# Weight parts in plain rows, read by the matmuls in passes over groups of eight or four

## The chip, the cores and the metric

The kernel runs on one core of a Trainium2 chip. The metric is the device time of one execution in microseconds; the median over several runs is compared. The trace and the page come from one profiled execution of the kernel before the change.

## The reference

With the sizes of this case (DEPTH = 1) only layer 0 and the last norm are computed: an RMS norm, a projection to q, k, v and gate, stick-breaking attention in 32 heads of 128, a gated output projection with a residual, and a final RMS norm. x is 256 x 4096, w_in 4096 x 16384, w_out 4096 x 4096, all float32.

```
def reference(x, norm_attn, w_in_attn, w_out_attn, ..., final_norm):
    h = x + attn_branch(rms_norm(x, norm_attn), w_in_attn, w_out_attn)
    return rms_norm(h, final_norm)

def attn_branch(xn, w_in, w_out):
    q, k, v, g = jnp.split(xn @ w_in, 4, axis=-1)
    o = stick_breaking_attention(to_heads(q), to_heads(k), to_heads(v))
    return (o * jax.nn.silu(g)) @ w_out

# per head, scores z = q k^T / sqrt(128), strictly causal:
#   log_a = log_sigmoid(z) + sum over later keys j < t of log_sigmoid(-z_tj)
#   o = exp(log_a) @ v
```

## The kernel before

**Numbers in two parts.** Every float32 operand of the two large projections is split into a high part (rounded to the float32r kind that the tensor engine takes in one pass) and a low part, the rest. `mm3` multiplies high x high, high x low and low x high: one *product* is three matmuls that add into the same PSUM bank. The activations (128 x 128 blocks, tiles sh and sl for the input side, oh and ol for the output side) are the stationary operand; a weight part (128 rows x 512 columns, tiles wh and wl) is the moving one.

**Units, steps, parts.** The work is cut into 20 units of 16 steps. Units 0 to 15 are the input projection (each gives two heads), units 16 to 19 the output projection. A step covers 256 rows of the reduction (two chunks of 128, c = 0 and 1) and two quadruples of column blocks. Units 0 and 16 are "plain" and make 8 products a step; the others save multiplications as in Strassen's scheme, with 7 products in ten of the steps (`SEVEN`) and 8 in the others. The sums of weight blocks that this needs are made by VectorE in place and by DMAs that add into the raw tiles (issued on POOL). In all there are 2383 products, 7149 matmuls of 512 columns.

**How a weight part is made.** SyncE loads a raw tile (`load`); ScalarE casts it to the high part and VectorE subtracts to get the low part (`piece`, `minus`). There are 7 raw tiles, 7 high and 5 low slots of full size, and two slots for singles, in which one chunk is formed and its high and low parts lie together.

**How a part lies and is read.** With `by_runs` a part of 1024 elements a partition lies in the order (h c i e): 64 groups h, in each the two chunks c, in each the two column blocks i, and last a run e of four elements. A matmul takes one chunk: it reads the runs of four that are 64 bytes apart, first all of block 0, then all of block 1, and writes its bank in order. Chunk 1 starts 32 bytes after chunk 0.

**What orders the work.** `Plan` is a simulated clock that the program runs while it is built: each engine has a queue of ready items with keys (due times), and an item is emitted when its engine is free in the simulation. So the order of instructions on every engine follows from cost formulas such as `tensor_ns` and `vector_ns`. `PRODUCT` is three times the tensor cost of 512 columns. The matmuls of the heads (transposes, scores, sums along a row, output) go through `ten`, between the products, with a key that puts them first.

**The output units.** `blocks_of_heads` forms the stationary parts of the output projection from the spilled results of the heads: it loads a block p on POOL's queue, casts it and subtracts. `later_than`, with SPREAD, says behind which step of the last input unit or of unit 16 each of these may begin.

Of the kernel before, what the change touches and what calls it, by code (L numbers as in the profile page):

```python
# [11 lines left out]
F32R = mybir.dt.float32r  # L12
# [7 lines left out]
P = 128  # L20
# [6 lines left out]
HG = CW // P  # L27
NB = D // CW
W = 2 * CW
NJ = D // W  # L30
KT = 2
NS = KC // KT
EPS = 1e-6

RUN = 4
WARM, IDLE = 10, 640


# [9 lines left out]
LOWS = 5  # L48
# [6 lines left out]
KEPT = 5  # L55
LAST_ORDER = (5, 4, 2, 3)

SPREAD = (12, 1.0)
HEADS_AHEAD = 0
SUMS_LATER = 2  # L60
H_LATER = 6
# [40 lines left out]


def tensor_ns(n):
    return 0.4167 * n + 12.4 if n > 128 else 109.0


class Plan:
# [135 lines left out]
def kernel(  # L244
# [10 lines left out]
    nc = Plan(tc)  # L255
# [3 lines left out]
    wp = ctx.enter_context(tc.tile_pool(name="weights", bufs=1))  # L259
# [10 lines left out]
    def minus(out_, full, part):  # L270
        nc.vector.tensor_tensor(out=out_, in0=full, in1=part.bitcast(F32), op=ALU.subtract)
# [30 lines left out]
    for b in LAST_ORDER:  # L302
        order += [(n, k) for n in kept for k, prod in enumerate(parts[n]["prods"]) if prod[0] == b]
    starts, ends, first, left, place_of = {}, {}, {}, {}, {}
    PRODUCT = 3 * tensor_ns(W)
    for g, (n, k) in enumerate(order):
        p = parts[n]
        b = p["u"], p["prods"][k][0]
# [16 lines left out]
    def dve(emit, n, key=None, more=0, **kw):  # L325
        n = n if isinstance(n, tuple) else (n,)
        cost = sum(vector_ns(m) for m in n) + 122 * (len(n) - 1) + more
        return nc.work("vector", cost, emit, soon() if key is None else key, **kw)

    def act(emit, n, key=None, **kw):  # L330
        n = n if isinstance(n, tuple) else (n,)
        cost = sum(scalar_ns(m) for m in n) + 100 * (len(n) - 1)
        return nc.work("scalar", cost, emit, soon() if key is None else key, **kw)


    FULL_P, FULL_S = (P,) * 2, (W,) * 2

    def ten(emit, *n):
        return nc.work("tensor", 40 + sum(tensor_ns(m) for m in n), emit, nc.here - 1e4, wait=400)

    def moved(engine, emit, sizes, key, after=None, hold=False, adds=False, wait=0):
        issue = 550 if engine == "gpsimd" else 330
# [17 lines left out]
    raw, wh, wl = {}, {}, {}  # L360
# [44 lines left out]
    def low_done(n):  # L405
        lows_left[n] -= 1
        if not lows_left[n]:
            nc.tell(("lows", n))
            tile_done(*parts[n]["tile"])

    def sums(q):

        a, b, c, d = quad_parts[q]
        one, two = raw[q, 0], raw[q, 1]
        for k in range(2):
            tile_left[q, k] += 1

        def add(to, at_, f, g, key, op=ALU.add):
            return dve(
                lambda: nc.vector.tensor_tensor(out=to[:, :, at_, :], in0=f, in1=g, op=op), W,  # L420
                key - SUMS_AHEAD * 1e3, more=120 if op == ALU.subtract else 10,
            )

        yield nc.until(("lows", a), ("T3", q))
        yield add(one, 0, one[:, :, 0, :], two[:, :, 0, :], first[c], ALU.subtract)
        yield nc.until(("lows", b))
        yield add(two, 1, one[:, :, 0, :], two[:, :, 1, :], first[c])
        nc.tell(("sums", c))
        yield add(one, 1, one[:, :, 0, :], one[:, :, 1, :], first[d])
        nc.tell(("sums", d))  # L430
        for k in range(2):
            tile_done(q, k)

    def by_runs(t):

        return t.rearrange("p (h c i e) -> p c i h e", c=KT, i=HG, e=RUN)

    def piece(n, c, there):

        p = parts[n]  # L440
        yield nc.until(*there)
        full = raw[p["tile"]][:, :, p["place"], :][:, :, c, :].rearrange("p i c (h e) -> p c i h e", e=RUN)
        h = wh[n][:, c]
        size = (c.stop - c.start) * W
        key = first[n] - (AHEAD * 1e3 if p["seven"] and p["i"] < 2 else 0)
        yield act(lambda: nc.scalar.copy(h, full), size, key - 2.0 * 1e3)
        if p["size"] == KT:
            if c.start == 0:
                yield nc.take("wl")
                wl[n] = by_runs(wp.tile([P, KT * W], F32R, tag="wl", name=f"wl{n}", bufs=LOWS))  # L450
                nc.tell(("lowslot", n))
            else:
                yield nc.until(("lowslot", n))
        l = wl[n][:, c]
        if n == 0:
            yield nc.until(("sh", c.start))
        yield dve(lambda: minus(l, full, h), size, key, more=10)
        for k in range(c.start, c.stop):
            nc.tell(("low", n, k))
        low_done(n)  # L460

    def split(size, tag, bufs):
        for n, p in enumerate(parts):
            if p["size"] != size:
                continue
            q = p["quad"]
            t = p["tile"][1]
            if size == KT:
                yield nc.take(tag)
            yield nc.until(("raw", q, t))  # L470
            if size < KT:
                yield nc.take(tag)
            wh[n] = by_runs(wp.tile([P, KT * W], F32R, tag="wh" if size == KT else "s", name=f"wh{n}", bufs=bufs))
            if size == 1:
                wh[n], wl[n] = wh[n][:, 0:1], wh[n][:, 1:2]
            cuts = [slice(k, k + 1) for k in range(KT)] if n == 0 else [slice(0, size)]
            lows_left[n] = len(cuts)
            if p["seven"] and p["i"] == 0:
                nc.start(sums(q))
            for c in cuts:  # L480
                nc.start(piece(n, c, [("sums", n)] if p["seven"] and p["i"] > 1 else [("raw", q, t)]))
# [312 lines left out]
        nc.give("gh")  # L794
        nc.tell(("gate", u))

    def mm3(out_, a, b, start, stop):

        (ah, al), (bh, bl) = a, b
        if len(bh.shape) == 4:  # L800
            out_ = out_.rearrange("p (i h e) -> p i h e", i=HG, e=RUN)
        kw = dict(skip_group_check=True)
        nc.tensor.matmul(out_, ah, bh, start=start, stop=False, **kw)
        nc.tensor.matmul(out_, ah, bl, start=False, stop=False, **kw)
        nc.tensor.matmul(out_, al, bh, start=False, stop=stop, **kw)


    BW = 3 * P
# [5 lines left out]
    def head(u, i):  # L814
# [3 lines left out]
        def turn():  # L818
            for k in range(2):
                for t in range(NT):  # L820
                    c = k * CW + i * P
                    nc.tensor.transpose(tr[:, k, t * P : (t + 1) * P], st["qk", u][:, t, c : c + P], ident)

        yield ten(turn, P, P, P, P)
        if i == HG - 1:
            nc.give("one")
# [6 lines left out]
        def scores():  # L833
            kw = dict(stop=False, skip_group_check=True)
            nc.tensor.matmul(z[:, 0:P], qk[:, 1, P:S], qk[:, 0, P:S], start=True, **kw)
            nc.tensor.matmul(z[:, P:BW], qk[:, 1, 0:P], qk[:, 0, :], start=False, **kw)

        yield ten(scores, *FULL_P, *FULL_S)
        nc.give("gh")
        yield nc.take("gh")  # L840
# [20 lines left out]
        def scan():  # L861
# [4 lines left out]
            nc.tensor.matmul(z[:, 2 * P : BW], neg_one, fl[:, 0:P], stop=True, **kw)  # L866

        yield ten(scan, BW, BW, P, P)
        nc.give("gh", "gh")
        yield nc.take("gh")  # L870
# [70 lines left out]
    def later_than(u, s):  # L941
        s = int(SPREAD[0] + SPREAD[1] * s)
        return "used", u + s // NS, s % NS
# [282 lines left out]
            nc.tell(("used", u, s))  # L1226

    def product(n, k):
        p = parts[n]
        b, f, c = p["prods"][k]  # L1230
        h, l = forms[p["s"]]
        mm3(
            ev[p["u"]][b],
            (h[:, PLACES[f], :], l[:, PLACES[f], :]),
            (wh[n][:, c], wl[n][:, c]),
            starts[p["u"], b] == (n, k),
            ends[p["u"], b] == (n, k),
        )

    def products():  # L1240
        for g, (n, k) in enumerate(order):
            p = parts[n]
            u, s = p["u"], p["s"]
            b, f, c = p["prods"][k]
            if u < 1:
                what = "s"
            elif u < OUT0:
                what = "n"
            elif u == OUT0:
                what = "o"  # L1250
            else:
                what = "r" if u == LAST and s in EIGHT_LAST else "p"
            if starts[u, b] == (n, k):
                yield nc.take(f"b{b}")
                ev.setdefault(u, {})[b] = acc.tile([P, W], F32, tag=f"b{b}", name=f"acc{u}_{b}")
            yield nc.until(("low", n, c), ("form", what, s), lead=nc.LEAD)
            yield nc.work(
                "tensor", PRODUCT, lambda: product(n, k), g * PRODUCT, after=lambda n=n, k=k: done(n, k), hold=False
            )
            nc.here = g * PRODUCT  # L1260

    together(split(KT, "w", HIGHS), split(1, "s", SINGLES), products(), x_stats(), x_factor(), constants())

    def in_turn(works):
# [55 lines left out]
```

## Time and profile before

| | |
|---|---|
| median of 3 runs | 1725.65 us (1722.67 to 1726.70) |
| the profiled execution | 1725.08 us, of which the span of its instructions is 1722.3 us |
| granted TensorE clock | 0.998 |
| busy: PE, PEld, DVE, ACT, POOL | 99%, 82%, 95%, 70%, 19% of the span |
| moved by DMA | 413.82 MB, mean 240 GB/s |

PE is the tensor engine's matmuls, PEld its weight loads, DVE VectorE, ACT ScalarE, POOL GpSimd. Matmuls overlap in the profile, since each begins before the one ahead has ended; the distance between two starts tells more than a duration. All of the kernel's operations are recorded through one helper, so they all stand under its line, L127, and are told apart by their tiles: wh and wl are the weight's parts, sh, sl, oh and ol the stationary blocks, acc the banks, raw the loaded weights, qk_sb, gv_sb, z, f and a the heads' tiles, p the spilled results that come back.

### The profile page before, as it was taken

What the parts mean: (1) busy time and instruction counts of PE and PEld (TensorE: products, weight loads), DVE (VectorE), ACT (ScalarE), POOL (GpSimd) and SP (SyncE); (2) the same over time, 40 slices, a digit from 0 to 9 for tenths busy, and PEclk for the clock granted to TensorE, in tenths of its full rate; (3) what the DMA queues carried; (4) which work ended last, traced back from release to release, by engine and by line L of the source; (5) the groups of instructions that cost most, each with busy time, mean ns of one, the idle gap of its engine ahead of it and who ended that gap; (6) DMA issues with size and microseconds to landing.
All of it is one profiled execution on the core that took longest, in us unless ns stands there. A gap on an engine that the chain in (4) does not pass through costs nothing. (4 is left out here: it accounts for less than half of the span.)

```text
span 1722.3 us, 25298 instructions
## 1 busy us (share of the span) xinstructions
PE 1704.4 (99%) x7735; PEld 1415.7 (82%) x7735; DVE 1634.9 (95%) x2106; ACT 1199.3 (70%) x1640; POOL 335.6 (19%) x407
## 2 busy tenths in 40 slices
PE   9999999999999999999999999999999999999997
PEld 7888888888888888888888888888888888878786
DVE  8899999999999999999999999999999978999997
ACT  8986767676767676767676767676767765666655
POOL 0012222222222222121212121212222112122120
PEclk9999999999999999999999999999999999999999
DMA  9978787878787979797978787878788978898895
GB/s 342 329 199 234 220 248 221 247 215 259 206 264 197 266 194 273 191 270 199 266 202 257 207 249 216 245 214 245 221 238 224 278 243 253 232 258 248 242 301 196
DMA packets 249384, 413.82 MB, mean 240 GB/s; under 512 B 28128, under 2 KB 73440, under 8 KB 249248
## 3 DMA queue, kind: packets, MB, share of 16 engines
q1 hardware_dynamic: 194544, 354.24, 62.2%
q0 software_dynamic: 54416, 57.70, 20.4%
q8 instruction: 60, 0.98, 0.2%
q14 instruction: 76, 0.62, 0.1%
q10 hardware_dynamic: 288, 0.28, 0.0%
HBM read 403.98 MB, written 8.13 MB: 239 GB/s over the span
## 5 line engine op out<-in xcount | busy, mean ns | idle before, releaser
L127 ACT CAST wh<-raw 128x1024 fp32r<-128x1024 f32 (+1 forms) x995 | 922.3, 969 | 412.2 <-DVE raw L127 207.3
L127 DVE TENSOR_TENSOR wl<-raw,wh 128x1024 fp32r<-128x1024 f32 (+1 forms) x818 | 974.9, 1218 | 33.7 <-PE acc L127 13.5
L127 PE MATMUL acc<-wh,sh 128*128 128x512 f32 x2048 | 783.5, 394 | 1.1 <-DVE qk_sb L127 0.7
L127 PE MATMUL acc<-wh,sl 128*128 128x512 f32 x1898 | 733.3, 386 | 0.0
L127 PE MATMUL acc<-wl,sh 128*128 128x512 f32 x1748 | 675.3, 386 | 0.0
L127 POOL DMA_DIRECT2D raw<-in_w_in_dram x300 | 263.1, 996 | 977.8 <-DMA raw<-in_w_in_dram 326.5
L127 PEld LDWEIGHTS acc<-wh,sh 128*128 128x128 f32 x2048 | 384.1, 188 | 77.9 <-issue 2.2
L127 PEld LDWEIGHTS acc<-wh,sl 128*128 128x128 f32 x1898 | 356.1, 188 | 73.4 <-DVE sl L127 0.5
L127 PEld LDWEIGHTS acc<-wl,sh 128*128 128x128 f32 x1748 | 328.5, 188 | 61.5 <-DVE wl L127 0.4
L127 DVE TENSOR_TENSOR raw<-raw,raw 128x512 f32<-128x512 f32 x354 | 242.6, 685 | 12.8 <-DMA raw<-in_w_in_dram 9.7
L127 PE MATMUL acc<-wh,oh 128*128 128x512 f32 x512 | 194.5, 388 | 0.0
L127 PE MATMUL acc<-wh,ol 128*128 128x512 f32 x485 | 187.1, 386 | 0.0
L127 PE MATMUL acc<-wl,oh 128*128 128x512 f32 x458 | 177.4, 387 | 3.8 <-DVE wl L127 3.8
L127 DVE TENSOR_TENSOR wh<-raw,wh 128x512 fp32r<-128x512 f32 x177 | 121.2, 684 | 1.3 <-ACT wh L127 1.3
L127 DVE TENSOR_TENSOR raw<-raw 128x512 f32<-128x512 f32 x177 | 121.0, 683 | 0.0
L127 PEld LDWEIGHTS acc<-wh,oh 128*128 128x128 f32 x512 | 96.0, 188 | 19.5 <-ACT wh L127 0.4
L127 PEld LDWEIGHTS acc<-wh,ol 128*128 128x128 f32 x485 | 90.9, 187 | 18.4
L127 PEld LDWEIGHTS acc<-wl,oh 128*128 128x128 f32 x458 | 85.8, 187 | 23.3 <-DVE wl L127 6.6
L127 POOL DMA_DIRECT2D raw<-in_w_out_dram x54 | 47.3, 976 | 182.1 <-DMA raw<-in_w_out_dram 65.9
L127 ACT ACTIVATE f<-f 128x384 f32<-128x384 f32 x96 | 50.5, 526 | 3.0
L127 ACT CAST oh<-p 128x512 fp32r<-128x512 f32 (+3 forms) x46 | 20.8, 467 | 23.5 <-DVE p L127 16.7
L127 POOL DMA_DIRECT2D p<-spill x28 | 17.0, 682 | 85.3 <-ACT gl L127 26.8
(83 smaller groups left out, 781.8 us busy)
## 6 DMA issues: line engine op xcount, KB each, us to landing
raw<-in_w_in_dram SPq DMA_DIRECT2D x1024, 256.0 KB, 4.5
raw<-in_w_out_dram SPq DMA_DIRECT2D x256, 256.0 KB, 4.4
raw<-in_w_in_dram POOLq DMA_DIRECT2D x300, 128.0 KB, 5.2
p<-spill POOLq DMA_DIRECT2D x28, 256.0 KB, 4.8
raw<-in_w_out_dram POOLq DMA_DIRECT2D x54, 128.0 KB, 5.3
xr<-in_x_dram SPq DMA_DIRECT2D x16, 256.0 KB, 5.4
xres<-in_x_dram SPq DMA_DIRECT2D x16, 256.0 KB, 6.2
out_dram<-h SPq DMA_DIRECT2D x16, 256.0 KB, 2.8
```

The costliest lines, as they stand in the source:

```text
L127: return self.tc.keep_in_program_order(getattr(self.engine, name)(*args, **kw))
```

## The change

Four things are changed. (1) A weight part lies in plain rows (c i n): chunk, block, column. (2) A matmul reads its 512 elements in `ROUNDS` = 4 passes: with order "e" each pass takes eight elements of every 32, with order "c" four elements of every 16. The output bank is addressed by the same pattern, so each element lands where it did. (3) Which of the two orders each matmul of a product takes is given by three letters: "eee" as a rule; the first two products behind a stretch of head matmuls take "ccc" and "ecc", and the first product of each step takes one of "cce", "ecc", "ccc" by the step's number. `since_others` counts the products since the last head matmuls. (4) Two constants: `tensor_ns` charges 8.5 ns over the columns in place of 12.4, and SPREAD begins at 10 in place of 12.

```
-RUN = 4
+ROUNDS = 4
+RUNS = {"e": 8, "c": 4}
+BEHIND_OTHERS = ("ccc", "ecc")
+IN_STEP = ("cce", "ecc", "ccc")
...
-SPREAD = (12, 1.0)
+SPREAD = (10, 1.0)
...
-    return 0.4167 * n + 12.4 if n > 128 else 109.0
+    return 0.4167 * n + 8.5 if n > 128 else 109.0
...
+    since_others = 0
+
     def ten(emit, *n):
-        return nc.work("tensor", 40 + sum(tensor_ns(m) for m in n), emit, nc.here - 1e4, wait=400)
+        def others():
+            nonlocal since_others
+            since_others = 0
+            emit()
+
+        return nc.work("tensor", 40 + sum(tensor_ns(m) for m in n), others, nc.here - 1e4, wait=400)
...
-    def by_runs(t):
-        return t.rearrange("p (h c i e) -> p c i h e", c=KT, i=HG, e=RUN)
+    def halves(t):
+        return t.rearrange("p (c i n) -> p c i n", c=KT, i=HG)
...
-        full = raw[p["tile"]][:, :, p["place"], :][:, :, c, :].rearrange("p i c (h e) -> p c i h e", e=RUN)
+        full = raw[p["tile"]][:, :, p["place"], :][:, :, c, :].rearrange("p i c n -> p c i n")
...
-    def mm3(out_, a, b, start, stop):
+    def mm3(out_, a, b, start, stop, orders):
         (ah, al), (bh, bl) = a, b
-        if len(bh.shape) == 4:
-            out_ = out_.rearrange("p (i h e) -> p i h e", i=HG, e=RUN)
-        kw = dict(skip_group_check=True)
-        nc.tensor.matmul(out_, ah, bh, start=start, stop=False, **kw)
-        nc.tensor.matmul(out_, ah, bl, start=False, stop=False, **kw)
-        nc.tensor.matmul(out_, al, bh, start=False, stop=stop, **kw)
+        for k, (x, y) in enumerate(((ah, bh), (ah, bl), (al, bh))):
+            to, y = (t.rearrange("p (h q e) -> p q h e", q=ROUNDS, e=RUNS[orders[k]]) for t in (out_, y))
+            nc.tensor.matmul(to, x, y, start=start and k == 0, stop=stop and k == 2, skip_group_check=True)
...
     def product(n, k):
+        nonlocal since_others
...
+        orders = "eee"
+        if since_others < len(BEHIND_OTHERS):
+            orders = BEHIND_OTHERS[since_others]
+        elif p["i"] == 0 and k == 0:
+            orders = IN_STEP[p["s"] % len(IN_STEP)]
+        since_others += 1
         mm3(
             ev[p["u"]][b],
             (h[:, PLACES[f], :], l[:, PLACES[f], :]),
-            (wh[n][:, c], wl[n][:, c]),
+            tuple(t[:, c].rearrange("p i n -> p (i n)") for t in (wh[n], wl[n])),
...
+            orders,
         )
```

More of the change, by code (lines that the diff above doesn't have):

```diff
@@ L449, in piece @@
                 yield nc.take("wl")
-                wl[n] = by_runs(wp.tile([P, KT * W], F32R, tag="wl", name=f"wl{n}", bufs=LOWS))
+                wl[n] = halves(wp.tile([P, KT * W], F32R, tag="wl", name=f"wl{n}", bufs=LOWS))
                 nc.tell(("lowslot", n))
@@ L472, in split @@
                 yield nc.take(tag)
-            wh[n] = by_runs(wp.tile([P, KT * W], F32R, tag="wh" if size == KT else "s", name=f"wh{n}", bufs=bufs))
+            wh[n] = halves(wp.tile([P, KT * W], F32R, tag="wh" if size == KT else "s", name=f"wh{n}", bufs=bufs))
             if size == 1:
```

## The prediction

> **What bounds the kernel now.** I read the page first, then the groups by form, then who waited for whom on the tensor engine, then stretches of one unit each, and last single matmul starts in the timeline.
>
> ```profile
> span 1722.3 us, 25298 instructions
> PE 1704.4 (99%) x7735; PEld 1415.7 (82%) x7735; DVE 1634.9 (95%) x2106; ACT 1199.3 (70%) x1640; POOL 335.6 (19%) x407
> PEclk9999999999999999999999999999999999999999
> L127 PE MATMUL acc<-wh,sh 128*128 128x512 f32 x2048 | 783.5, 394 | 1.1 <-DVE qk_sb L127 0.7 <-ACT wh L127 0.4
> L127 PE MATMUL acc<-wh,sl 128*128 128x512 f32 x1898 | 733.3, 386 | 0.0
> L127 PE MATMUL acc<-wl,sh 128*128 128x512 f32 x1748 | 675.3, 386 | 0.0
> L127 PE MATMUL acc<-wh,oh 128*128 128x512 f32 x512 | 194.5, 388 | 0.0
> L127 PE MATMUL acc<-wh,ol 128*128 128x512 f32 x485 | 187.1, 386 | 0.0
> L127 PE MATMUL acc<-wl,oh 128*128 128x512 f32 x458 | 177.4, 387 | 3.8 <-DVE wl L127 3.8
> PE acc L127 <- DVE wl L127: 3.8, 3, 1.9
> ```
>
> The tensor engine is busy 99% of the span at full clock and its longest wait on anybody adds up to 3.8 us. The six groups are the products: 2048+1898+1748+512+485+458 = 7149 matmuls of 512 columns, 2383 products of three. Their mean durations (386 to 394 ns) overlap, so they are not the price; the price is the distance from one start to the next. VectorE stands right behind at 95%. Stretches of one unit (unit 1, unit 5, unit 16, unit 17, unit 19; columns are busy us and instruction counts of PE, PEld, DVE, ACT, POOL):
>
> ```profile
> 95.45:180.05 84.60, 84.60 (x389) 70.75 (x388) 80.21 (x98) 61.23 (x82) 17.80 (x21) 1.00 0.82 230
> 434.89:519.89 85.00, 85.00 (x391) 71.00 (x390) 82.70 (x102) 60.27 (x80) 17.99 (x21) 1.00 0.81 232
> 1371.18:1463.28 92.10, 91.94 (x422) 76.59 (x421) 73.52 (x128) 58.00 (x93) 16.51 (x27) 1.00 0.77 243
> 1463.28:1546.06 82.78, 80.86 (x356) 66.11 (x354) 80.95 (x101) 52.11 (x67) 15.83 (x19) 1.00 0.87 247
> 1628.52:1710.85 82.33, 82.27 (x364) 67.76 (x362) 77.80 (x110) 47.88 (x67) 10.06 (x12) 1.00 0.75 231
> ```
>
> A middle unit with heads takes 85.00 us, and VectorE works 82.70 of them (97.3%): 2.3 us of slack a unit, no more. In unit 17 (and 18 like it), which has no heads, TensorE is busy only 80.86 of 82.78 and VectorE 97.8%: that unit already waits for VectorE. So two engines are near their limit together: TensorE sets the pace in most units, VectorE in units 17 and 18.
>
> Now the price of one matmul. A stretch without heads (unit 7, steps 7 to 15), one step behind heads (unit 5, step 1), both with the instructions on acc alone, and four products of one step in the timeline (start, duration):
>
> ```profile
> 645.21:689.81 44.60, 44.60 (x199) 37.10 (x198) 2.02 (x3) 1.26 (x2) 1.00 0.91 269
> 441.44:446.27 4.83, 4.83 (x22) 3.96 (x21) 0.00 (x0) 0.00 (x0) 1.00 0.42 141
> 654.67 0.38 PE L127 MATMUL acc<-wh,sh 128*128 128x512 f32 x1
> 654.89 0.38 PE L127 MATMUL acc<-wl,sh 128*128 128x512 f32 x1
> 655.11 0.39 PE L127 MATMUL acc<-wh,sl 128*128 128x512 f32 x1
> 655.34 0.38 PE L127 MATMUL acc<-wh,sh 128*128 128x512 f32 x1
> 655.56 0.39 PE L127 MATMUL acc<-wl,sh 128*128 128x512 f32 x1
> 655.78 0.39 PE L127 MATMUL acc<-wh,sl 128*128 128x512 f32 x1
> 656.02 0.39 PE L127 MATMUL acc<-wh,sh 128*128 128x512 f32 x1
> 656.24 0.38 PE L127 MATMUL acc<-wl,sh 128*128 128x512 f32 x1
> 656.47 0.38 PE L127 MATMUL acc<-wh,sl 128*128 128x512 f32 x1
> 656.68 0.40 PE L127 MATMUL acc<-wh,sh 128*128 128x512 f32 x1
> 656.92 0.39 PE L127 MATMUL acc<-wl,sh 128*128 128x512 f32 x1
> 657.15 0.38 PE L127 MATMUL acc<-wh,sl 128*128 128x512 f32 x1
> 657.37 0.38 PE L127 MATMUL acc<-wh,sh 128*128 128x512 f32 x1
> ```
>
> 44.60/198 = 225.3 ns is the undisturbed mean; 4.83/21 = 230 ns is a step behind heads. In the timeline the first and third products (chunk 0) take 0.67 and 0.66 us, the second and fourth (chunk 1) 0.68 and 0.69: 1.33/6 = 222 ns against 1.37/6 = 228 ns a matmul. Both kinds have the same shape, the same kind of stationary tile, the same order of three; what differs is where the moving operand lies: 32 bytes further on within each 64. So the order in which the weight part is read has a price, 6 ns in 225, and no other engine's work is needed to explain it.
>
> **The change part by part.** *Reads.* Before, each matmul reads runs of four elements, 64 bytes apart, in two passes, and writes its bank in order. After, it reads a plain row in four passes, each of sixteen runs of eight 128 bytes apart ("e") or thirty-two runs of four 64 bytes apart ("c"), and the bank is written in the same broken order. No row shows "e" or a broken write, so the price is bounded. From above: the 228 ns of chunk 1, and for a read that is wholly in order the two matmuls of 384 columns of the heads:
>
> ```profile
> 616.86 0.34 PE L127 MATMUL z<-fh,neg_tri 128*128 128x384 f32 x1
> 617.03 0.34 PE L127 MATMUL z<-fl,neg_tri 128*128 128x384 f32 x1
> 617.21 0.22 PE L127 MATMUL z<-fh,neg_tri 128*128 128x128 f32 x1
> 617.27 0.27 PE L127 MATMUL z<-fl,neg_tri 128*128 128x128 f32 x1
> ```
>
> (617.21-616.86)/2 = 175 ns for 384, against 60 for 128: 0.45 ns a column, so 512 in order would be 175+128*0.45 = 233 ns. From below: the shortest start-to-start of the twelve, 656.47 to 656.68, 0.21 us as rounded, so between 0.20 and 0.22; I use 217. I take 221.8: the new layout puts both chunks at the same place within any 128 bytes (a chunk is 2 KB), so chunk 1 loses its offset, which speaks for the 222 of chunk 0; and the planner's own charge, in the old code 0.4167 ns a column and 12.4 (225.7, between the 225.3 and 230 above), is set to 0.4167 and 8.5 (221.8). Gain 3.5 ns a matmul against 225.3; 7149 of them are 25.0 us if nothing else binds. Ends: -8 ns (gain) and +8 ns (loss).
>
> *The group-of-four passes* go to one product of each step and up to two behind each stretch of head matmuls, the places where the row above shows 230 instead of 225. Cost or gain is inside the bounds given; I count nothing extra.
>
> *Writes of the parts.* ScalarE's cast and VectorE's subtraction now write rows instead of runs. VectorE:
>
> ```profile
> L127 DVE TENSOR_TENSOR wl<-raw,wh 128x1024 fp32r<-128x1024 f32 x816 | 973.5, 1219 | 33.6 <-PE acc L127 13.5 <-ACT wh L127 11.4 <-ACT sh L127 1.0
> L127 DVE TENSOR_TENSOR raw<-raw,raw 128x512 f32<-128x512 f32 x354 | 242.6, 685 | 12.8 <-DMA raw<-in_w_in_dram 9.7 <-DMA raw<-in_w_out_dram 0.8
> L127 DVE TENSOR_TENSOR wh<-raw,wh 128x512 fp32r<-128x512 f32 x177 | 121.2, 684 | 1.3 <-ACT wh L127 1.3
> ```
>
> 512 elements into runs (wh) take 684 ns, into rows (raw) 685, so the layout is free there: nothing gained. ScalarE has 30% to spare; nothing either way.
>
> *Planner constants.* The cheaper product shifts the simulated times, so the order on every queue may change in places. SPREAD 12 to 10 lets the first conversion of the heads' results for the output units begin two steps earlier: each is a spill load (p, on POOL's queue), a ScalarE cast and a VectorE subtraction plus sums, and two more of them (about 1.4 us of VectorE, at the 0.685 us row twice) fall into unit 15 rather than 16. POOL is 19% busy; what is queued behind them there is the next raw accumulate, wanted steps later. VectorE in unit 16 has 18 us of slack, in unit 15 as little as in unit 5. I charge 0.5 us, inside the loss below.
>
> *The sum, with VectorE as the second bound.* A middle unit (354 matmuls) would go from 85.00 to 83.76 us (354 x 3.5 ns = 1.24) and VectorE's share to 82.70/83.76 = 98.7%. The highest share any unit shows is 97.8%, with TensorE waiting. So part of the gain is lost there: I take 0.24 of the 1.24 us. Units 2 to 15: 14 x 1.0 = 14.0. Unit 1 (VectorE 94.8%): 1.24. Units 0 and 16 (384 matmuls, VectorE with slack): 1.34 each. Unit 19 (363): 1.27. Units 17 and 18, already waiting for VectorE: 0.3 each, since a faster TensorE only waits longer. Total 19.8 us. The profiled execution took 1725.08 us, span 1722.3 and 2.8 around it; 1725.08 - 19.8 = 1705.3, given as 1705. The median of the runs is 1725.65, so nothing is to be shifted for that.
>
> **The rivals.** *VectorE takes over (1714).* If 97.8% is the most it can be driven to, a middle unit cannot go under 82.70/0.978 = 84.56 us: 14 x 0.44 = 6.2 us there, nothing in 17 and 18, and 1.24+2.68+1.27 = 5.2 elsewhere, 11.4 in all. For it: the row of unit 17. Against: the waits of VectorE's subtraction for acc (13.5 us), that is for a slot that TensorE frees, shrink when TensorE is faster.
>
> *A larger gain (1696).* At 217 ns everywhere a middle unit would be limited by VectorE alone; at 98.7% it still gains 1.2 us, 17 in fourteen units, and the others some 3 each: 29 us. Nothing says that all matmuls reach the best interval of today's cycle.
>
> *No change (1725).* The intervals might belong to the weight loads (1415.7 us of PEld lie under the matmuls) or to a rhythm of TensorE that no read order alters; then the change does not do what it says. Against: 222 against 228 with equal weight loads.
>
> *Slower by the residues (1746).* In the old layout chunk 1 reads only the upper 32 of each 64 bytes; in the new one two of every matmul's four passes do. If a pass there holds up the whole matmul, all matmuls cost 228.3: 7149 x 3.0 = 21 us more. It decides as soon as the mean exceeds 225.3. For it: only half of today's matmuls are free of those addresses. Against: the first matmul of chunk 1 takes 0.22 us in one product (655.34 to 655.56) and 0.24 in the next but one (656.68 to 656.92), at like addresses, so the address alone isn't the price.
>
> *Slower by the broken write (1930).* The write to the bank is in order today and has 64 breaks ("e") or 128 ("c") after. If each break cost one column's 0.45 ns, a matmul would take 29 ns more, 7149 x 28.6 = 204 us; from 0.06 ns a break (3.5/64) the gain is gone. No row shows a broken write. The Trainium skill, PSUM — Partial Sum Buffer, Specifications (TRN2), speaks for this one: lines are 8 bytes, and any access that is not contiguous slows matmuls significantly; it gives no figure. Advanced Engine Details and Errata, Memory Cachelines, narrows it: two consecutive elements should stay together, which runs of four and eight do; by that reading this rival falls. Runs of four in the read, which are no contiguous access either, cost less here (222 to 228) than the in-order 384-column row implies (233).
>
> **How the numbers follow.** Forecast 0.48 (own range 1699 to 1710), VectorE takes over 0.20, larger gain 0.12, no change 0.06, residues 0.09, broken write 0.05. Runs of this kernel can tell 0.2%, 3.5 us. Faster: 0.80; same: 0.06; slower: 0.14. The range leaves the slower cases out and reaches from a little beyond the larger gain to no change: 1690 to 1726.
>
> **What would show it.** Right: the distance of product starts falls to about 222 in a stretch without heads, no more gap between chunk 0 and 1; VectorE's share in middle units above 98%, with its subtraction still at 1219 ns and more waits of acc for wl than 3.8 us; units 17 and 18 nearly unmoved at 82.5. Wrong: a mean interval at or above 225, or a middle unit still near 85 us although the intervals are short.

## The result and the profile after

The changed kernel takes 1740.01 us (median; 1738.70 to 1747.36), the kernel before 1725.65. The ratio is 1.0098 with a 95% interval of 1.0073 to 1.0123: slower by 1%, where 1705 was forecast. First the page of the changed kernel (its helper line is now L130): span, engines and what the groups waited for.

```profile
span 1737.5 us, 25252 instructions
...
PE 1692.8 (97%) x7735; PEld 1413.9 (81%) x7735; DVE 1629.7 (94%) x2106; ACT 1205.4 (69%) x1640; POOL 336.2 (19%) x407
...
L130 PE MATMUL acc<-wh,sh 128*128 128x512 f32 x2048 | 780.7, 393 | 22.6 <-DVE qk_sb L130 19.7
...
L130 DVE TENSOR_TENSOR raw<-raw,raw 128x512 f32<-128x512 f32 x354 | 244.2, 690 | 47.0 <-DMA raw<-in_w_in_dram 42.9
```

Both engines do less in a longer span: PE went from 1704.4 to 1692.8 us, DVE from 1634.9 to 1629.7. What grew are two idle times. TensorE waits 19.7 us for qk_sb, the adds with which VectorE empties the banks at the end of a unit; before it waited 0.7. VectorE waits 42.9 us for raw, the weights to which a DMA adds a second block; before 9.7.

The matmuls themselves became faster. Here is the same stretch without heads (unit 7, steps 7 to 15, busy time of the instructions on acc):

```profile
651.48:695.13 43.65, 43.65 (x199) 37.07 (x198) 2.04 (x3) 1.27 (x2) 1.00 0.86 245
```

And some matmul starts of it in the timeline:

```profile
687.21 0.38 PE L130 MATMUL acc<-wh,sh 128*128 128x512 f32 x1
687.43 0.38 PE L130 MATMUL acc<-wl,sh 128*128 128x512 f32 x1
687.65 0.38 PE L130 MATMUL acc<-wh,sl 128*128 128x512 f32 x1
687.87 0.38 PE L130 MATMUL acc<-wh,sh 128*128 128x512 f32 x1
688.09 0.38 PE L130 MATMUL acc<-wl,sh 128*128 128x512 f32 x1
688.31 0.38 PE L130 MATMUL acc<-wh,sl 128*128 128x512 f32 x1
688.53 0.38 PE L130 MATMUL acc<-wh,sh 128*128 128x512 f32 x1
```

43.65/198 = 220.5 ns a start, where it was 225.3; every distance shown is 0.22 us, and the gap between chunk 0 and chunk 1 is gone. Now the stretches of units 1, 5, 16, 17 and 19, with the columns as in the prediction:

```profile
94.63:177.92 83.29, 83.29 (x389) 70.72 (x388) 79.55 (x99) 61.14 (x81) 16.63 (x20) 1.00 0.81 231
437.24:525.03 87.79, 85.89 (x390) 72.32 (x391) 83.56 (x104) 61.73 (x81) 18.15 (x21) 0.98 0.82 231
1387.52:1481.85 94.33, 91.73 (x421) 76.49 (x420) 74.98 (x130) 58.81 (x94) 15.62 (x25) 1.00 0.75 236
1481.85:1563.68 81.83, 79.73 (x355) 66.15 (x354) 79.00 (x97) 50.98 (x66) 15.84 (x19) 1.00 0.86 246
1644.49:1725.08 80.59, 80.59 (x364) 67.72 (x362) 76.64 (x107) 47.77 (x67) 10.10 (x12) 1.00 0.74 229
```

Unit 1 gains 1.31 us and unit 19 1.7, more than forecast. Unit 17 gains 0.95 us. Unit 16 loses 2.2 us, and unit 5, a middle one, loses 2.8 us (85.00 to 87.79). The timeline of VectorE in unit 3 and at the start of unit 5 shows how (start, duration; idle before and what ended it in brackets):

```profile
314.46 0.69 DVE L130 TENSOR_TENSOR raw<-raw,raw 128x512 f32<-128x512 f32 x1
318.18 0.69 DVE L130 TENSOR_TENSOR raw<-raw,raw 128x512 f32<-128x512 f32 x1 [3.02 <-DMA raw<-in_w_in_dram]
...
334.80 0.69 DVE L130 TENSOR_TENSOR raw<-raw,raw 128x512 f32<-128x512 f32 x1 [2.03 <-DMA raw<-in_w_in_dram]
...
438.81 1.22 DVE L130 TENSOR_TENSOR wl<-raw,wh 128x1024 fp32r<-128x1024 f32 x1
439.94 0.75 DVE L130 SCALAR_TENSOR_TENSOR qk_sb<-acc,scalars,qk_sb 128x512 f32<-128x512 f32 x1
```

And the timeline of TensorE at the start of unit 5:

```profile
438.45 0.39 PE L130 MATMUL acc<-wh,sl 128*128 128x512 f32 x1
440.74 0.50 PE L130 MATMUL acc<-wh,sh 128*128 128x512 f32 x1 [1.90 <-DVE qk_sb L130]
...
443.07 0.63 PE L130 MATMUL acc<-wh,sl 128*128 128x512 f32 x1
443.50 0.63 PE L130 MATMUL acc<-wh,sh 128*128 128x512 f32 x1
```

Late in unit 3 VectorE stands still for 3.02 and 2.03 us in front of a sum whose transfer has not landed; in unit 4 the same waits are 1.42 and 2.26 us. Nothing else runs on it meanwhile (between 315.15 and 318.18 it is empty), so the subtractions and the adds that the program lists behind the sum are late. At the start of unit 5 TensorE needs a bank that such an add (qk_sb, 439.94) has not yet freed, and stops for 1.90 us. Once in this execution the stop also brings the clock to half: 0.43 us from start to start at 443. The mean granted clock of the five executions is 0.991 to 0.996; in the run with 12.4 of the next section, which has hardly any such stops, it is 0.997 or 0.998 in all four. So lower clock behind the stops is a part of the loss; how large a part was not measured.

### The profile page after: what moved, and what is told of

It is laid out like the page before. It is cut to its first block, busy times and chain, and to the rows that moved or that the text cites. A ratio compares the mean times of both kernels' runs of the same rounds, so it can differ in the third digit from the quotient of the medians.

```text
span 1737.5 us, 25252 instructions
## 1 busy us (share of the span) xinstructions
PE 1692.8 (97%) x7735; PEld 1413.9 (81%) x7735; DVE 1629.7 (94%) x2106; ACT 1205.4 (69%) x1640; POOL 336.2 (19%) x407
## 4 chain that ended last, share of the span: by engine, by line
PE 81%; DVE 8%; DMA 5%; issue 4%; ACT 1%; SPq 0%; DVEq 0%; POOL 0%; POOLq 0%; ACTq 0%
PE acc L130 77%; DMA raw<-in_w_in_dram 4%; DVE wl L130 4%; PE z L130 2%; DVE raw L130 2%; PE o L130 1%; DVE qk_sb L130 1%; PE tr L130 1%; ACT wh L130 1%; DMA p<-spill 0%; DVE h L130 0%; DVE wh L130 0%; DMA xres<-in_x_dram 0%; DVE gv_sb L130 0%; SPq L130 0%
## 5 line engine op out<-in xcount | busy, mean ns | idle before, releaser
L130 ACT CAST wh<-raw 128x1024 fp32r<-128x1024 f32 (+1 forms) x995 | 922.9, 971 | 428.7 <-DVE raw L130 223.7
L130 DVE TENSOR_TENSOR wl<-raw,wh 128x1024 fp32r<-128x1024 f32 (+1 forms) x818 | 973.8, 1221 | 31.0 <-ACT wh L130 15.4
L130 PE MATMUL acc<-wh,sh 128*128 128x512 f32 x2048 | 780.7, 393 | 22.6 <-DVE qk_sb L130 19.7
L130 PE MATMUL acc<-wh,sl 128*128 128x512 f32 x1898 | 730.4, 385 | 1.1 <-DVE sl L130 1.1
L130 PE MATMUL acc<-wl,sh 128*128 128x512 f32 x1748 | 671.5, 384 | 1.1 <-DVE wl L130 1.0
L130 PEld LDWEIGHTS acc<-wh,sh 128*128 128x128 f32 x2048 | 383.6, 188 | 100.6 <-DVE qk_sb L130 25.5
L130 POOL DMA_DIRECT2D raw<-in_w_in_dram x300 | 263.1, 990 | 990.4 <-DMA raw<-in_w_in_dram 480.0
L130 PEld LDWEIGHTS acc<-wh,sl 128*128 128x128 f32 x1898 | 356.2, 188 | 69.2 <-DVE sl L130 1.8
L130 PEld LDWEIGHTS acc<-wl,sh 128*128 128x128 f32 x1748 | 328.6, 188 | 59.9 <-DVE wl L130 3.1
L130 DVE TENSOR_TENSOR raw<-raw,raw 128x512 f32<-128x512 f32 x354 | 244.2, 690 | 47.0 <-DMA raw<-in_w_in_dram 42.9
L130 PE MATMUL acc<-wh,oh 128*128 128x512 f32 x512 | 193.0, 385 | 0.2 <-DVE gv_sb L130 0.2
L130 PE MATMUL acc<-wh,ol 128*128 128x512 f32 x485 | 186.1, 384 | 0.0
L130 PE MATMUL acc<-wl,oh 128*128 128x512 f32 x458 | 176.4, 385 | 3.7 <-DVE wl L130 3.7
L130 DVE TENSOR_TENSOR wh<-raw,wh 128x512 fp32r<-128x512 f32 x177 | 121.9, 689 | 0.1
L130 DVE TENSOR_TENSOR raw<-raw 128x512 f32<-128x512 f32 x177 | 121.6, 687 | 0.0
L130 PEld LDWEIGHTS acc<-wh,oh 128*128 128x128 f32 x512 | 96.0, 188 | 18.3 <-DVE gv_sb L130 0.6
L130 PEld LDWEIGHTS acc<-wh,ol 128*128 128x128 f32 x485 | 90.9, 188 | 16.5
L130 PEld LDWEIGHTS acc<-wl,oh 128*128 128x128 f32 x458 | 85.9, 188 | 22.0 <-DVE wl L130 6.4
L130 POOL DMA_DIRECT2D raw<-in_w_out_dram x54 | 47.4, 982 | 175.3 <-DMA raw<-in_w_out_dram 88.7
L130 ACT ACTIVATE f<-f 128x384 f32<-128x384 f32 x96 | 50.6, 527 | 3.0
L130 POOL DMA_DIRECT2D p<-spill x28 | 17.1, 669 | 89.4 <-DVE ol L130 51.1
L130 DVE SCALAR_TENSOR_TENSOR gv_sb<-acc,scalars,gv_sb 128x512 f32<-128x512 f32 x45 | 33.8, 751 | 0.0
```

The source lines that it names most:

```text
L130: return self.tc.keep_in_program_order(getattr(self.engine, name)(*args, **kw))
```

## The experiments

Each ratio is to the kernel before, measured on the same chip in the same set of runs.

**The two halves of the change.** The plan (order of all engines' instructions) follows from `tensor_ns` and SPREAD alone, since the way `mm3` reads does not enter it. So reads and plan can be had one without the other. First the new layout and reads with the old plan:

```
-    return 0.4167 * n + 8.5 if n > 128 else 109.0
+    return 0.4167 * n + 12.4 if n > 128 else 109.0
-SPREAD = (10, 1.0)
+SPREAD = (12, 1.0)
```

> The changed kernel with the planner's two old constants (12.4 and SPREAD 12), so every engine has the order of the kernel before and only the layout and the reads are new. Plan theory (the reads are faster as the trace of after shows, 222.6 ns a start instead of 225.5, and the order written with 8.5 loses it at the units' starts): 1704 to 1713 us, stalls over 260 ns back to about 1 us a middle unit. Feed theory (TensorE now outruns VectorE and the loads, whatever the order): stalls of 3 us a unit stay, 1728 to 1742 us.

1710.47 us, ratio 0.9928 (0.9914 to 0.9943): the reads gain 13 us. Its VectorE waits 9.8 us for accumulated tiles. Then the kernel before with the new plan (the same two lines in the other direction):

> The kernel before with the planner's two new constants (8.5 and SPREAD 10), reads and layout as before. Plan theory: the order alone makes units wait at their start also with slow reads; 1738 to 1765 us. Feed theory: TensorE is as slow as before, so nothing outruns anything; 1722 to 1729 us.

1735.55 us, 1.0077 (1.0064 to 1.0089): the plan alone costs 12 us, with the old reads, a little under the range that the plan theory gave.

VectorE's longest wait in that run, in the list of waits (total in us, times, longest):

```profile
DVE raw L127 <- DMA raw<-in_w_in_dram: 32.7, 27, 2.9
```

The feed theory falls: TensorE was as slow as before and VectorE stood still all the same. The two halves do not add up to the whole (-13 and +12 against +14): with the faster reads the same order costs more, 29 us (1740.01 against 1710.47).

**Which constant.** The changed kernel with SPREAD 12, and with 12.4:

> The changed kernel with SPREAD back at 12 and 8.5 kept; the order differs only from unit 15 on. Both theories: unit 15 (VectorE 85.1 us of work against 82.8 before) and unit 16 (94.3 against 92.1 us, a wait of 2.4 us of tr for gated) get back what they lost, up to 4 us: 1735 to 1740; the stalls of units 3 to 14 stay. If SPREAD were the whole cause: 1705 to 1712.

> The changed kernel with 12.4 back and SPREAD kept at 10. Plan theory with the tensor cost as its main part: within 4 us of the kernel with both constants old, 1705 to 1716. Feed theory: 1728 to 1742.

With 8.5 and SPREAD 12: 1746.21 us, 1.0150 (1.0130 to 1.0170). I had expected a gain of up to 4 us from it and it lost 6 us against the change by the medians, 9 by the ratios: the unit of the output projection's first blocks, 16, takes 105.81 us there. Its stretch, and TensorE's second wait in the list of waits:

```profile
1381.82:1487.63 105.81, 95.74 (x421) 78.07 (x420) 79.56 (x138) 61.57 (x98) 16.74 (x27) 0.95 0.69 220
```

```profile
PE acc L130 <- ACT oh L130: 6.0, 2, 5.7
```

So with 8.5, SPREAD 10 is no part of the loss but softens it. With 12.4 and SPREAD 10: 1707.96 us, 0.9910 (0.9897 to 0.9923), not to be told from 12.4 and SPREAD 12 (0.9928). The whole loss hangs on 8.5 against 12.4.

**Is it the wait for the accumulated tiles?** The changed kernel, with the planner told of the landing 2 us later:

```
+LATE = 2000
-        yield nc.until(("lows", a), ("T3", q))
+        yield nc.until(("lows", a))
+        yield nc.until(("T3", q), lead=LATE)
```

> The changed kernel with one thing altered in the planner: it takes the accumulated raw tile to be there 2 us later than it otherwise reckons, so VectorE's order has the sums further back. Blocked-queue theory (with 8.5 the sums stand in VectorE's order before their accumulating transfer has landed, VectorE, which works in order, stands still for it 43 us, and what is queued behind, the subtractions and the adds that free the banks, is late): the wait of raw for its transfer falls from 42.9 to under 15 us and the time to 1708 to 1720. Supply theory (the transfers themselves come late because the raw slots come free late; the wait is a symptom): the wait moves to TensorE, 1730 to 1745.

1713.61 us, 0.9949 (0.9933 to 0.9966); the wait of raw is 11.8 us, and TensorE's wait for qk_sb falls from 19.7 to 3.2 us. Then the accumulating transfers left out, once with 8.5 and once with 12.4:

```
-                nc.gpsimd.dma_start(r[:, i, 0, :], w[c, s][:, 1, :], accum_op=ALU.add)
+                pass
```

> The changed kernel without the accumulating transfers (the sums use the raw tile as loaded, so the values of seven-product steps are others); order of all engines as in the changed kernel. Blocked-queue theory: with nothing to wait for at the sums the whole loss goes: 1690 to 1706 us, no wait over 2 us at a unit's start, granted clock 0.998. If the loss lies elsewhere in that order (the adds that free the banks simply stand too late in it): 1725 to 1740.

> The same without the accumulating transfers, with 12.4 in the planner: the partner of the run above, for what the missing transfers alone bring. Blocked-queue theory: VectorE's waits for these transfers are only 15.6 us here, so it gains 2 to 8 us on 1708: 1700 to 1706, and the two orders come within 6 us of each other. Otherwise the order with 8.5 stays 20 us behind this one.

1706.41 us with 8.5 (0.9904; 0.9886 to 0.9923) and 1704.80 with 12.4 (0.9891; 0.9869 to 0.9912). Without the transfers the two orders are alike; with them they are 32 us apart (1740.01 and 1707.96). Leaving them out also lightens the DMAs' load, but that brings the order with 12.4 only 3 us, so it is not what cures the other. The stretch of unit 5 in the run with 8.5:

```profile
430.65:514.87 84.22, 84.22 (x391) 70.91 (x390) 82.50 (x102) 60.44 (x80) 0.54 (x1) 1.00 0.62 203
```

84.22 us with VectorE at 98%: the order with 8.5 is not too dense for VectorE. What it cannot bear is a transfer that lands after VectorE has come to its sum.

**Where.** The two waits in unit 3 end 56 and 73 us after its start (262.11), and VectorE works about a step ahead of TensorE, with some 5.4 us a step: that points to the sums of steps 11 and 14. The other units agree: in units 2 to 15 one wait ends 53 to 57 us after the unit's start and another 69 to 73 (units 5 and 15 have the first alone). The same delay of 2 us, first in these two steps alone, then in the other eight alone:

```
-        yield nc.until(("lows", a), ("T3", q))
+        yield nc.until(("lows", a))
+        yield nc.until(("T3", q), lead=2000 if parts[a]["s"] in (11, 14) else 0)
```

> The changed kernel (8.5, SPREAD 10), with the accumulated tile reckoned 2 us later in steps 11 and 14 alone. If the loss comes from the sums of these two steps: VectorE's wait for accumulated tiles from 42.9 to under 20 us and 1708 to 1720 us. If the plan is too short everywhere: 1728 to 1742.

> The partner: 2 us later in the other eight seven-product steps, not in 11 and 14. If the loss comes from steps 11 and 14: nothing is cured, 1730 to 1745 us, waits for accumulated tiles stay above 30 us. If any slack in the plan would do: 1708 to 1722.

Late at 11 and 14: 1715.30 us, 0.9949 (0.9932 to 0.9966). Late elsewhere: 1738.96, 1.0091 (1.0068 to 1.0114). VectorE's sums in the groups by form of the two runs, the cured one first:

```profile
L130 DVE TENSOR_TENSOR raw<-raw,raw 128x512 f32<-128x512 f32 x354 | 242.1, 684 | 14.4 <-DMA raw<-in_w_in_dram 9.6 <-DMA raw<-in_w_out_dram 2.1
```

```profile
L130 DVE TENSOR_TENSOR raw<-raw,raw 128x512 f32<-128x512 f32 x354 | 241.9, 683 | 42.4 <-DMA raw<-in_w_in_dram 39.7 <-DMA raw<-in_w_out_dram 0.6 <-DVE raw L130 0.4
```

TensorE's wait for qk_sb is 0.9 us in the first and 19.6 in the second. So the sums of two steps a unit, placed in VectorE's order a little too near to their transfer, carry most of the loss: delaying them brings as much as delaying all ten (0.9949 both times). What keeps these two runs some 7 us behind 12.4 (0.9910) was not tried, nor why it is these two steps.

**Other figures in the plan.**

> The changed kernel with 10.5 ns in the planner in place of 8.5 (between the two). Blocked-queue theory, loss growing as the planned unit gets shorter than VectorE and the transfers can follow: VectorE waits 20 to 30 us for accumulated tiles, 1712 to 1726 us. If any figure below today's is as bad: 1735 to 1742. If 8.5 is merely an unlucky order: 1705 to 1711.

> The changed kernel with 15.0 ns in the planner: a plan slower than TensorE is. Blocked-queue theory: VectorE waits still less for accumulated tiles (under 15 us), the time stays at 1704 to 1712. If the planner's figure should simply equal what TensorE does, 15 is as wrong as 8.5 is right, and this loses: 1720 or more.

> 12.4 in the planner and the accumulated tiles reckoned 1 us later, both cures at once, as a candidate for the fastest version. Blocked-queue theory: the 15.6 us that VectorE still waits in the run with 12.4 alone fall to under 10; 1703 to 1708 us, 0 to 5 us under it.

10.5 gives 1706.31 us (0.9902; 0.9887 to 0.9917), 15.0 gives 1705.26 (0.9903; 0.9888 to 0.9918), 12.4 with the tiles reckoned 1 us later 1708.34 (0.9915; 0.9902 to 0.9929). I had expected a loss that grows with the shorter plan; there is none down to 10.5, so it begins somewhere between 10.5 and 8.5. The later tiles bring nothing on top of 12.4, although VectorE's wait for them falls from 15.6 to 7.1 us. All of these beat both kernels and cannot be told from each other. With 10.5, the line of the list of waits and the stretch of unit 6:

```profile
DVE raw L130 <- DMA raw<-in_w_in_dram: 3.7, 7, 1.2
```

```profile
513.26:597.10 83.84, 83.84 (x392) 70.87 (x391) 82.44 (x102) 60.73 (x80) 17.92 (x21) 1.00 0.84 235
```

**What the reads cost.** All with 12.4 and SPREAD 10. In one pass in order; all reads in eights; fours only behind head matmuls; all reads in fours:

```
-            to, y = (t.rearrange("p (h q e) -> p q h e", ...) for t in (out_, y))
-            nc.tensor.matmul(to, x, y, ...)
+            nc.tensor.matmul(out_, x, y, ...)
```

> Weight parts in plain rows, read and written in one pass in order (no groups), with 12.4 in the planner: the price of the read order. The prediction's estimate from the 384-column row is 233 ns a start; then a middle unit takes 354 x 11 ns = 3.9 us more than with the groups and TensorE is the bound again: 1770 to 1785 us. If the order of reading does not matter: 1705 to 1712.

```
-BEHIND_OTHERS = ("ccc", "ecc")
-IN_STEP = ("cce", "ecc", "ccc")
+BEHIND_OTHERS = ("eee", "eee")
+IN_STEP = ("eee", "eee", "eee")
```

> The changed kernel with 12.4 in the planner and every read in groups of eight (no groups of four anywhere): the partner of the run with 12.4 and SPREAD 10 at 1708 us. If the groups of four bring TensorE back into its short intervals behind the heads and at a step's start: mean interval up from 222.0 to 223.5 or more, 1714 to 1722 us. If they are beside the point: intervals within 0.3 ns of 222.0, 1705 to 1711.

```
-IN_STEP = ("cce", "ecc", "ccc")
+IN_STEP = ("eee", "eee", "eee")
```

> The changed kernel with 12.4, SPREAD 10 and groups of four only in the two products behind head matmuls, not at each step's start. If a rhythm once entered lasts until the next head matmuls: mean interval within 1 ns of the 222.0 of the kernel with both, 1705 to 1716 us. If it must be renewed at each step: 226 to 230 ns, 1725 to 1748.

```
-BEHIND_OTHERS = ("ccc", "ecc")
-IN_STEP = ("cce", "ecc", "ccc")
+BEHIND_OTHERS = ("ccc", "ccc")
+IN_STEP = ("ccc", "ccc", "ccc")
...
-        orders = "eee"
+        orders = "ccc"
```

> The changed kernel with 12.4, SPREAD 10 and groups of four in every read. If fours are the fast read: 218 to 222 ns, 1700 to 1710 us. If it is the change between the two orders that keeps the rhythm, fours alone are as slow as eights alone (230 ns): 1730 to 1750 us.

The stretch of unit 7, steps 7 to 15, on acc, in order, in eights, in fours, and in eights with fours only behind heads (198 starts in each):

```profile
649.67:694.55 44.88, 44.88 (x199) 37.16 (x198) 2.02 (x3) 1.28 (x2) 1.00 0.91 267
```

```profile
656.50:702.17 45.67, 45.67 (x199) 37.28 (x198) 2.03 (x3) 1.26 (x2) 1.00 0.91 264
```

```profile
645.35:690.21 44.86, 44.86 (x199) 37.13 (x198) 2.02 (x3) 1.27 (x2) 1.00 0.93 268
```

```profile
636.41:679.97 43.56, 43.56 (x200) 37.09 (x199) 2.02 (x3) 1.25 (x2) 1.00 0.91 270
```

| reads | ns a start in that stretch | us, ratio |
|---|---|---|
| before: fours, two passes | 44.60/198 = 225.3 | 1725.65 |
| in order | 44.88/198 = 226.7 | 1733.23, 1.0062 (1.0043 to 1.0082) |
| all eights | 45.67/198 = 230.7 | 1748.29, 1.0148 (1.0134 to 1.0161) |
| all fours | 44.86/198 = 226.6 | 1724.60, 1.0002 (0.9992 to 1.0011) |
| eights, fours behind heads | 43.56/198 = 220.0 | 1711.28, 0.9933 (0.9916 to 0.9950) |
| eights, fours at both places | 220.5 (in the change) | 1707.96, 0.9910 (0.9897 to 0.9923) |

In order, 233 ns and 1770 to 1785 us were expected from the 384-column row of the prediction: the estimate was 6 ns too high. The eights alone are far worse than the 223.5 ns and 1714 to 1722 us that I expected, and the fours alone lie between the two answers that I had put up.

Neither eights nor fours are the fast read. Eights run in two rhythms, one at 220 ns and one at 230.7 (distances of 0.23 and 0.24 us), with the same reads. A few fours behind the head matmuls bring them into the short rhythm, and it lasts until the next interruption. Without fours they run in the long one in all middle units, but not everywhere. Here is a place of unit 17 in the run with all eights, and a stretch behind it:

```profile
1545.05 0.39 PE L130 MATMUL acc<-wh,ol 128*128 128x512 f32 x1
1545.28 0.39 PE L130 MATMUL acc<-wh,oh 128*128 128x512 f32 x1
1545.84 0.50 PE L130 MATMUL acc<-wl,oh 128*128 128x512 f32 x1 [0.16 <-DVE wl L130]
...
1547.78 0.38 PE L130 MATMUL acc<-wh,oh 128*128 128x512 f32 x1
1548.00 0.38 PE L130 MATMUL acc<-wl,oh 128*128 128x512 f32 x1
```

```profile
1555.48:1566.92 11.44, 11.44 (x53) 9.74 (x52) 2.00 (x3) 1.08 (x2) 1.00 0.99 303
```

Ahead of a wait of 0.16 us the distance is 0.23 us, soon behind it 0.22: 11.44/52 = 220.0 ns, with no four in the kernel. So an interruption alone can change the rhythm.

It can do so the other way as well. In the run with fours only behind heads the units without heads take 83.10 and 83.73 us at the end against 81.05 and 81.46 of the run with fours at both places (units 18 and 19): a stop of 1.88 us at 1505.44 ends the short rhythm there, and the long one then lasts to the end. What makes the two rhythms (the weight loads, the read of the moving operand, the write to the bank) was not tried.

## Why the prediction was wrong, point by point

**The price of a matmul** was right in size: 220.5 ns in the undisturbed stretch, 221.8 forecast. The reason given was not. I argued that chunk 1 loses its offset; the kernel with all eights has the same layout, no offset, and needs 230.7, and with all fours, where no chunk has an offset either, it is 226.6. The value came out because the fours bring in the short rhythm, which the prediction did not know of: that the size was right was luck.

**The groups of four** were counted at nothing. They decide over 10 ns a matmul in most of the kernel: leaving them out costs 40 us (1748.29 against 1707.96).

**VectorE as the second bound** was right: with an order that suits, a middle unit takes 83.84 to 84.2 us with VectorE at 98.3% (82.44 of 83.84), where 84.0 and 98.7% were forecast, and unit 17 does not gain (83.01 with 10.5, 82.78 before). Two terms were off: unit 18 gains 1.4 us (81.05 with 12.4, 82.46 before) where 0.3 was reckoned, and unit 16 loses 2 us (94.06 with 12.4, 92.10 before) where a gain of 1.34 was. With 10.5 the whole gains 16.4 us of the 19.8 that the sum gave.

**The planner's constants** are the step that failed. "I charge 0.5 us, inside the loss below": the plan costs 12 us with the old reads and 29 with the new (1740.01 against 1710.47), the tensor cost alone 32 with the new (1740.01 against 1707.96). I took the order as a matter of places here and there, and priced SPREAD, which in fact helped; the part that mattered was the tensor cost. It puts sums of VectorE ahead of the landing of their transfers, VectorE stands still for 42.9 us, and TensorE then waits for banks. The row that could have warned me stood in the prediction: VectorE's sums waited 9.7 us for DMAs even before, and with 2.3 us of slack a unit nothing was left to make such a wait good.

**The rivals.** None of them was what came. Nearest was "VectorE takes over": it does so, not by its work but by standing still in order. "Slower by the residues" comes near in time (1746) and is wrong in mechanism: it asks for a mean above 225.3, and the mean fell. "No change" supposed a rhythm that no read order alters; there is a rhythm, but the reads do alter it. The broken write did not bring the loss that its rival priced: eights, which break the write and the read alike, reach 220.5 ns, and the in-order run needs 226.7. No run broke the write alone, so a small price of it stays possible. The Trainium skill, PSUM — Partial Sum Buffer, Specifications (TRN2), which has any access that is not contiguous slow matmuls significantly, does not agree with these numbers. The Trainium skill, Advanced Engine Details and Errata, Memory Cachelines, says the same of the bank, and adds that every two consecutive elements should lie together for the best throughput; runs of four and eight keep to that second sentence.

## What to carry to other kernels

When the order on in-order queues is computed from a cost model, a constant of it is part of the schedule: price a change of it like a change of code, and test it alone. With two engines as near to their limits as here, a truer figure for one engine made a worse order (8.5 charges 221.8 ns, and 220.5 were measured), for it placed work right behind transfers that then landed a little late; a figure further on the slow side left the slack that these transfers needed and cost nothing (10.5, 12.4 and 15.0 within 3 us). And a kernel that is faster in its inner loop can hide the gain under one blocked queue: look at what each engine waited for, not at busy shares, which here went down on both.

## What was not expected of the hardware

The distance of back-to-back matmuls of 512 columns took two stable values, 220 and 230.7 ns, with the same reads. Reads in fours right before set the short one (220.0 against 230.7 in unit 7), but a wait of 0.16 us did so too; what decides is not known. A stop of TensorE of 2.3 us from start to start (438.45 to 440.74, 1.90 us shown as idle) was followed by matmuls at half clock. Two stretches of 1 us there (the third number from the end is the granted clock):

```profile
441.00:442.00 1.00, 1.00 (x6) 0.84 (x6) 1.00 (x3) 0.00 (x0) 0.00 (x0) 0.84 0.94 147
442.00:443.00 1.00, 1.00 (x4) 0.89 (x4) 1.00 (x2) 0.96 (x2) 0.00 (x0) 0.50 0.83 125
```

The Trainium skill, TensorE: Matmul & The Clock Gate, Why this matters for your kernels, puts the limit at gaps of about 3 us; here 2.3 were enough once, while stops of like length at other units of the same execution (1.92 us shown as idle at 353.48, 2.14 at 1216.79) left the clock at 1.00.
